# A hybrid attention layer on one core: product tails, decay ranks and block sums in another order

## The chip, the core and the metric

The kernel runs on one core of a Trainium2 chip. A core has a matmul engine (PE, whose weight loads are shown as PEld), a vector engine (DVE), a scalar engine (ACT), a general engine (POOL), a queue engine (SP) that mostly issues DMAs, and 16 DMA engines. Every engine works through its own queue in order and waits on semaphores where it needs another's result. The metric is the device time of one execution in microseconds; lower is better. Three executions of the kernel before took 2083.85 to 2084.41 us, median 2084.07 us.

## What is computed

One layer, in float32, on 1024 tokens of width 1024: a half-step SwiGLU feed-forward (width 2816), a mixer, and a second half-step feed-forward, each followed by a scaled residual and a layer norm.

```
x = layer_norm(ALPHA * x + 0.5 * swiglu_ffn(x, ffn1...), ln1)
x = layer_norm(ALPHA * x + hybrid_mixer(x, ...), ln2)
x = layer_norm(ALPHA * x + 0.5 * swiglu_ffn(x, ffn2...), ln3)

swiglu_ffn: (silu(x @ w_gate) * (x @ w_up)) @ w_down
hybrid_mixer: proj = x @ w_in -> na_q, na_k, na_v, g_q, g_k, g_v, g_g, dec_f, dec_b, gates
  merged = sigmoid(gate_na) * (neighborhood_attention(na_q, na_k, na_v) @ w_branch_na)
         + sigmoid(gate_gla) * (gated_linear_attention(g_q, g_k, g_v, g_g, dec_f, dec_b) @ w_branch_gla)
  return merged @ w_out
```

The two decay ranks `dec_f` and `dec_b` are 16 columns of the input projection each; they feed the decay gates of the linear attention.

## The kernel before, in words

Tokens are kept transposed: eight blocks of 128 model columns by two halves (h = 0, 1) of 512 tokens. Every float32 operand is split into a rounded high part and a low rest (`split`: an ACT copy and a DVE subtraction), and every product is three matmuls per block: high x high, high x low, low x high.

**Two-by-two products.** Most of the feed-forward and of the input projection is done by a Strassen-Winograd scheme: seven products of half size instead of eight. The token side is the 2 x 2 block matrix b11, b12 (blocks 0 to 3, half 0 and 1) and b21, b22 (blocks 4 to 7). Its sums t1 = b12 - b11, t2 = b22 - t1, t3 = b22 - b12 and t4 = b21 - t2 are made once per stage by `sums_of(i)` for i = 0 to 3, one block of each of the four sums at a time: four DVE subtractions and four splits per call. The results are T[0] to T[3]. The weight side is made per item by `factors`: `a11`, `a12`, `a22`, `s1` to `s4`.

**The order on PE.** PE's queue is exactly the order in which the program text issues matmuls (a manual schedule for this engine). For the other engines a list scheduler orders the instructions by priority, which is program order, and moves those inside `hoist()` or `high_priority` forward by 100 places. A second, hand-kept clock (`at`, `run`) places norm and attention steps between matmul steps.

**`blocks` and `pairs`.** `blocks` (L565) makes the gate and up projections of the feed-forward tiles 2 to 21; `pairs` (L884) makes eight items of the input projection. Both pipeline items: for item n the order is a11, a12 | `s3` of item n-1 | `s1` x T[0], `s2` x T[1] | `a22` of item n-1 | `s4`. `s3` and `a22` accumulate into one bank X; between them DVE adds the bank to a saved value (L587 in `blocks`, L936 in `pairs`). For the last item the loop runs once more with no new item, so its `s3`, the DVE read and its `a22` follow one another. `dense` has four PSUM banks.

**`down`, `deferred`.** The down projection (L712) does the same for eight items (two groups of six row tiles, four m each), with `gather` (L681) as the DVE read. The `s1` and `s4` products of the last two items, m = 2 and 3, are put on a list `wait`; `deferred` (L758) runs them later, behind the first of the parts that handle the remaining tiles (`plain` over LAST, L653): both `s1`, then both `s4`. Ahead of `down`, `front` runs 16 products over four other tiles.

**Between FFN1 and the pairs.** `tok_major` (L857) makes the attention values token-major: eight tiles of 128 tokens, of 24 matmuls (L873 to L875) each. Tiles 0 to 3 read half 0 of the normalized tokens, tiles 4 to 7 half 1, whose norm is still being finished meanwhile: DVE applies it (L322, L323), ACT scales and rounds, POOL subtracts the low part (L412). Then come the sums and `decay_rank` (L959): per half 16 matmuls (L970 to L973) into one bank, a copy, an addition (L977), a split and three stores. Its weights are loaded, rounded and split (L964) at its start. Then `pairs` begins, and behind it neighbourhood attention (L1077 and L1079 scores, L1083 to L1088 softmax, L1097 transposes) among the matmuls of a second `tok_major`.

Of the kernel before, what the change touches and what calls it, by code (L numbers as in the profile page):

```python
# [1 line left out]

# [7 lines left out]
F32R = mybir.dt.float32r  # L10
BF16 = mybir.dt.bfloat16
U32 = mybir.dt.uint32
AF = mybir.ActivationFunctionType
ALU = mybir.AluOpType
# [4 lines left out]
P = 128  # L19
D = 1024  # L20
S = 1024
KD = D // P
# [45 lines left out]
def hybrid_layer(ctx, tc, xT, wg1, wu1, wds1, wd1, wg2, wu2, wds2, wd2, wcol, wnv, wgv, wdl, wgate,  # L68
                 wbr, wout, lnp, bias, dec2, bdec, ng, ident_d, masks_d, ln3, outN):
    nc = tc.nc  # L70
# [56 lines left out]
    def dps(shape=(P, HF)):  # L127
        return dense.tile(list(shape), F32, tag="d", name=nm("d"))

    def split(src, hi, lo):  # L130
        nc.scalar.activation(hi, src, AF.Copy)  # L131
        nc.vector.tensor_tensor(lo, src, hi.bitcast(F32), ALU.subtract)  # L132
# [4 lines left out]
    def atile(dt=F32):  # L137
        return apool.tile([P, HF], dt, tag="a", name=nm("a"))
# [23 lines left out]
    for c1 in FIRST:  # L162
        w = slice(c0 * P, c1 * P)
# [25 lines left out]
    def run(*streams):  # L189
        for st_ in streams:  # L190
            for cost in st_:
                clock[0] += cost
                while pending and pending[0][0] <= clock[0]:
                    pending.pop(0)[2]()
# [6 lines left out]
    def hoist():  # L201
        return tc.high_priority(offset=HOIST)
# [228 lines left out]
    class Ffn:  # L431
# [16 lines left out]
                    self.hp.tile([P, HF], F32R, tag="hl", name=nm("hl")))  # L448


        def sums_of(self, i):
            b11, b12 = self.xr[i]
            b21, b22 = self.xr[i + 4]
            t1, t2, t3, t4 = (self.sr() for _ in range(4))
            outs = [self.hpair(), self.hpair()]
            nc.vector.tensor_tensor(t1, b12, b11, ALU.subtract)
            split(t1, *outs[0])
            nc.vector.tensor_tensor(t2, b22, t1, ALU.subtract)
            split(t2, *outs[1])
            nc.vector.tensor_tensor(t3, b22, b12, ALU.subtract)  # L460
            nc.vector.tensor_tensor(t4, b21, t2, ALU.subtract)
            outs += [(atile(F32R), atile(F32R)) for _ in range(2)]
            split(t3, *outs[2])
            split(t4, *outs[3])
            for n in range(4):
                self.T[n][i] = outs[n]


        def glu(self, f, ws, h):
# [95 lines left out]
        def blocks(self, fs):  # L565
            x, T = self.x, self.T
            b11, b21, b22 = ([x[k + o][h] for k in range(4)]
                             for o, h in ((0, 0), (4, 0), (4, 1)))
            prev = None
            for f in [*fs, None]:  # L570
                if f is not None:
                    w = self.factors(self.wg[f], self.wu[f])
                    X = dps()
                    yield from self.product(X, w["a11"], b11, True)
                    s1 = self.tmp()
                    with hoist():
                        nc.scalar.activation(s1, X, AF.Copy)
                    Y = dps()
                    yield from self.product(Y, w["a12"], b21, True)
                    with hoist():  # L580
                        nc.vector.tensor_tensor(s1, Y, s1, ALU.add)
                        nc.scalar.activation(s1, s1, AF.Silu)
                if prev:
                    g, pX, p1, p2, p5, pw = prev
                    yield from self.product(pX, pw["s3"], T[2])
                    with hoist():
                        nc.vector.tensor_tensor(p5, pX, p5, ALU.add)  # L587
                        nc.vector.tensor_tensor(p2, p2, p5, ALU.mult)
                    self.hidden(g, 1, p2)
                if f is not None:  # L590
                    Z = dps()
                    yield from self.product(Z, w["s1"], T[0], True)
                    s5 = self.tmp()
                    with hoist():
                        nc.scalar.activation(s5, Z, AF.Copy)
                    yield from self.product(X, w["s2"], T[1])
                    s2 = self.tmp()
                    with hoist():
                        nc.scalar.activation(s2, X, AF.Copy)
                if prev:  # L600
                    yield from self.product(pX, pw["a22"], T[3])
                    with hoist():
                        nc.vector.tensor_tensor(p1, pX, p1, ALU.mult)
                    self.hidden(g, 0, p1)
                if f is not None:
                    yield from self.product(Z, w["s4"], b22)
                    with hoist():
                        nc.vector.tensor_tensor(s2, Z, s2, ALU.add)
                        nc.scalar.activation(s2, s2, AF.Silu)
                    prev = f, X, s1, s2, s5, w  # L610


        def operands(self, j0):
# [98 lines left out]
        def down(self):  # L712
            prev, B, nxt = None, None, self.operands(0)
            self.wait = []
            items = [(j0, m) for j0 in range(0, PAIRS, NP) for m in range(4)]
            for it in [*items, None]:
                if it:
                    j0, m = it
                    if m == 0:
                        B, nxt = nxt, None  # L720
                    w = self.down_factors(j0, m)
                    if m == 1:
                        if j0 + NP < PAIRS:
                            nxt = self.operands(j0 + NP)
                        else:
                            for f in LAST:
                                self.fetch(f, 0)
                    X = dps()
                    yield from self.product(X, w["a11"], B[0], True)
                    self.gather(2 * m, 0, X)  # L730
                    Y = dps()
                    yield from self.product(Y, w["a12"], B[1], True)
                    self.gather(2 * m, 0, Y)
                if prev:
                    pm, pX, pw, pB = prev
                    yield from self.product(pX, pw["s3"], pB[5])
                    self.gather(2 * pm + 1, 1, pX)
                late = it and j0 + NP == PAIRS and m > 1
                if late:
                    self.wait.append((m, w, B))  # L740
                elif it:
                    Z = dps()
                    yield from self.product(Z, w["s1"], B[3], True)
                    self.gather(2 * m + 1, 1, Z)
                if it:
                    yield from self.product(X, w["s2"], B[4])
                    self.gather(2 * m, 1, X)
                if prev:
                    yield from self.product(pX, pw["a22"], pB[6])
                    self.gather(2 * pm + 1, 0, pX)  # L750
                if it:
                    if not late:
                        yield from self.product(Z, w["s4"], B[2])
                        self.gather(2 * m, 1, Z)
                    prev = m, X, w, B


        def deferred(self):  # L758
            banks = []
            for m, w, B in self.wait:  # L760
                banks.append(dps())
                yield from self.product(banks[-1], w["s1"], B[3], True)
                self.gather(2 * m + 1, 1, banks[-1])
            for Z, (m, w, B) in zip(banks, self.wait):
                yield from self.product(Z, w["s4"], B[2])
                self.gather(2 * m, 1, Z)

# [5 lines left out]
        def go(self, first, parts, sink_of):  # L773
# [5 lines left out]
                w2.append(ws)  # L779
            for f in (0, 1):  # L780
                run(self.glu(f, w2[f], 1))
            for i in range(4):
                self.sums_of(i)
            run(self.blocks(range(head, FT)))
            self.front()
            run(self.down())
# [1 line left out]
            sums = tagged(self.hp, ("sr",), 4)  # L788
# [33 lines left out]
    one = Ffn(ffn1, x, xr, half(xT), wg1, wu1, wds1, wd1, 0)  # L822
# [61 lines left out]
    def pairs(mb, items, each, last):  # L884
# [31 lines left out]
        for it in [*items, None]:  # L916
# [15 lines left out]
            if prev:  # L932
                g, pX, p5, pw = prev
                yield from mb.product(pX, pw["s3"], T[2])
                with hoist():
                    nc.vector.tensor_tensor(p5, pX, p5, ALU.add)  # L936
                store(g[3], 1, p5)
            if it:
                Z = dps()
# [10 lines left out]
                with hoist():  # L950
                    store(g[3], 0, pX, mb.tmp())
            if it:
                yield from mb.product(Z, w["s4"], b22)
                with hoist():
                    nc.vector.tensor_tensor(s2, Z, s2, ALU.add)
                store(it[2], 1, s2)
                prev = it, X, s5, w

    def decay_rank():  # L959
        raw = wpool.tile([P, KD, 32], F32, tag="raw", name=nm("raw"), bufs=2)  # L960
# [19 lines left out]
            for i, t in enumerate((hi, lo, hi)):  # L980
                nc.sync.dma_start(dls[32 * i:32 * i + 32, h * HF:(h + 1) * HF], t[0:32])

    run(tok_major(wnv, lambda t: vscr[t * P:(t + 1) * P, :], one.hpair))
    assert not pending
    x1h = [[x1[k][h] for k in range(KD)] for h in range(2)]
    one.x, one.xr = x1, x1r
    for i in range(4):
        one.sums_of(i)
    run(decay_rank())
    wq = []  # L990


# [527 lines left out]
```

## Time and profile before

| what | before |
|---|---|
| median of three runs | 2084.07 us |
| profiled execution | 2085.47 us |
| its span (first to last instruction) | 2083.6 us |
| matmuls | 9722 |
| PE busy | 2048.2 us |
| DVE busy | 1382.0 us |
| ACT busy | 898.5 us |
| POOL busy | 165.4 us |
| DMA moved | 321.37 MB |

Line numbers (L559) are lines of the kernel before. In a timeline the columns are start, duration, engine, line, operation and tiles, and in brackets the idle time just before and what ended it. Matmuls overlap: one is drawn as 0.39 us, though the next may start long before it ends, so a loss of time is best read from the distance of the starts. In a table of stretches the columns are the stretch, its length, busy time and number of instructions of PE, PEld, DVE, ACT and POOL, the granted clock of PE as a share of full speed, the busy share of the DMA engines and GB/s. In the list of waits they are total, number and longest.

### The profile page before, as it was taken

What the parts mean: (1) busy time and instruction counts of PE and PEld (TensorE: products, weight loads), DVE (VectorE), ACT (ScalarE), POOL (GpSimd) and SP (SyncE); (2) the same over time, 40 slices, a digit from 0 to 9 for tenths busy, and PEclk for the clock granted to TensorE, in tenths of its full rate; (3) what the DMA queues carried; (4) which work ended last, traced back from release to release, by engine and by line L of the source; (5) the groups of instructions that cost most, each with busy time, mean ns of one, the idle gap of its engine ahead of it and who ended that gap; (6) DMA issues with size and microseconds to landing.
All of it is one profiled execution on the core that took longest, in us unless ns stands there. A gap on an engine that the chain in (4) does not pass through costs nothing.

```text
span 2083.6 us, 26748 instructions
## 1 busy us (share of the span) xinstructions
PE 2048.2 (98%) x9722; PEld 1684.4 (81%) x9722; DVE 1382.0 (66%) x2356; ACT 898.5 (43%) x1503; POOL 165.4 (8%) x252
## 2 busy tenths in 40 slices
PE   9999999999999999989999999999999999999997
PEld 7888888888888788867778888887888888888887
DVE  8676776457668965236557765799767776457647
ACT  6444444322224654336655544455544444312222
POOL 0000000000013221222100000033000000000001
PEclk9999999999999999999999999999999999999999
DMA  4443444396641354477553335422334443496622
GB/s 145 147 155 141 167 142 138 125 312 216 220 136 55 108 199 145 128 194 228 160 139 106 107 127 182 142 81 71 137 137 152 165 160 120 126 333 216 236 90 82
DMA packets 159764, 321.37 MB, mean 154 GB/s; under 512 B 18448, under 2 KB 42768, under 8 KB 159632
## 3 DMA queue, kind: packets, MB, share of 16 engines
q1 hardware_dynamic: 139664, 271.93, 38.7%
q0 software_dynamic: 9856, 31.47, 5.3%
q10 hardware_dynamic: 10112, 16.26, 2.5%
q8 instruction: 77, 1.26, 0.2%
q14 instruction: 55, 0.45, 0.1%
HBM read 222.19 MB, written 101.06 MB: 155 GB/s over the span
## 4 chain that ended last, share of the span: by engine, by line
PE 84%; issue 6%; DVE 4%; DMA 2%; POOL 2%; ACT 1%; SPq 0%; ACTq 0%; POOLq 0%; DVEq 0%
PE d L559 16%; PE d L561 16%; PE d L560 16%; PE d L122 6%; PE d L124 6%; PE d L123 6%; PE d L660 3%; PE d L661 3%; PE d L659 3%; PE pt L1097 1%; PE po L1114 1%; DMA gv<-sl 1%; PE d L875 1%; PE d L874 1%; PE d L873 1%
## 5 line engine op out<-in xcount | busy, mean ns | idle before, releaser
L131 ACT ACTIVATE wh<-raw 128x512 fp32r<-128x512 f32 (+4 forms) x148 | 111.7, 764 | 191.8 <-PE d L560 87.0
L132 DVE TENSOR_TENSOR wl<-raw,wh 128x512 fp32r<-128x512 f32 (+4 forms) x148 | 125.2, 854 | 102.0 <-ACT wh L131 101.8
L681 DVE TENSOR_TENSOR a<-a,d 128x512 f32<-128x512 f32 (+1 forms) x152 | 100.0, 658 | 90.3 <-PE d L561 60.7
L123 PE MATMUL d<-xl,wh 128*128 128x512 f32 x384 | 150.6, 392 | 3.6 <-POOL xl L412 3.1
L122 PE MATMUL d<-xh,wh 128*128 128x512 f32 x384 | 153.6, 400 | 0.5 <-ACT xh L131 0.3
L559 PE MATMUL d<-a,wh 128*128 128x512 f32 x384 | 149.8, 390 | 2.4 <-DVE hr L587 1.6
L124 PE MATMUL d<-xh,wl 128*128 128x512 f32 x384 | 150.4, 392 | 0.5 <-DVE wl L112 0.5
L561 PE MATMUL d<-hh,hl 128*128 128x512 f32 x384 | 149.5, 389 | 0.0
L561 PE MATMUL d<-xh,wl 128*128 128x512 f32 x384 | 149.5, 389 | 0.0
L560 PE MATMUL d<-a,wh 128*128 128x512 f32 x384 | 149.4, 389 | 0.0
L561 PE MATMUL d<-a,wl 128*128 128x512 f32 x384 | 149.4, 389 | 0.0
L560 PE MATMUL d<-xl,wh 128*128 128x512 f32 x384 | 149.4, 389 | 0.0
L560 PE MATMUL d<-hl,hh 128*128 128x512 f32 x384 | 149.4, 389 | 0.0
L559 PE MATMUL d<-xh,wh 128*128 128x512 f32 x384 | 149.4, 389 | 0.0
L559 PE MATMUL d<-hh,hh 128*128 128x512 f32 x384 | 149.4, 389 | 0.0
L131 ACT ACTIVATE hh<-sr 128x512 fp32r<-128x512 f32 x168 | 106.1, 632 | 83.0 <-DVE sr L500 23.8
L659 PE MATMUL d<-hh,wh 128*128 128x512 f32 (+1 forms) x368 | 134.3, 365 | 0.0
L661 PE MATMUL d<-hh,wl 128*128 128x512 f32 (+1 forms) x368 | 133.0, 361 | 0.0
L660 PE MATMUL d<-hl,wh 128*128 128x512 f32 (+1 forms) x368 | 133.0, 361 | 0.0
L132 DVE TENSOR_TENSOR hl<-sr,hh 128x512 fp32r<-128x512 f32 x168 | 115.0, 698 | 2.0 <-ACT hh L131 1.2
L112 DVE TENSOR_TENSOR wl<-raw,wh 128x512 fp32r<-128x512 f32 (+1 forms) x77 | 81.2, 1054 | 51.8 <-ACT wh L111 46.1
L111 ACT ACTIVATE wh<-raw 128x512 fp32r<-128x512 f32 (+1 forms) x77 | 67.7, 879 | 103.4 <-PE d L123 38.3
(335 smaller groups left out, 4901.2 us busy)
## 6 DMA issues: line engine op xcount, KB each, us to landing
raw<-in_wu SPq DMA_DIRECT2D x44, 512.0 KB
raw<-in_wg SPq DMA_DIRECT2D x43, 512.0 KB
ops<-oh SPq DMA_DIRECT2D x84, 256.0 KB
ops<-ol SPq DMA_DIRECT2D x84, 256.0 KB
oh<-ops SPq DMA_DIRECT2D x48, 256.0 KB
ol<-ops SPq DMA_DIRECT2D x48, 256.0 KB
hid<-oh SPq DMA_DIRECT2D x40, 256.0 KB
hid<-ol SPq DMA_DIRECT2D x40, 256.0 KB
```

The source lines that it names most:

```text
L122: nc.tensor.matmul(ps, a, xh, start=k == 0, stop=False)
L123: nc.tensor.matmul(ps, a, xl, start=False, stop=False)
L124: nc.tensor.matmul(ps, wl[:, k * m:(k + 1) * m], xh, start=False, stop=k == n - 1)
L131: nc.scalar.activation(hi, src, AF.Copy)
L132: nc.vector.tensor_tensor(lo, src, hi.bitcast(F32), ALU.subtract)
L559: nc.tensor.matmul(ps, a, xh, start=first and k == 0, stop=False, **sg)
L560: nc.tensor.matmul(ps, a, xl, start=False, stop=False, **sg)
L561: nc.tensor.matmul(ps, wl[:, k * P:(k + 1) * P], xh, start=False, stop=k == n - 1, **sg)
L659: nc.tensor.matmul(ps, wh, hi, start=k == 0, stop=False)
L660: nc.tensor.matmul(ps, wh, lo, start=False, stop=False)
L661: nc.tensor.matmul(ps, wl, hi, start=False, stop=k == n - 1)
L681: nc.vector.tensor_tensor(a, a, ps, ALU.add)
```

## The change

Four orders are changed; no product is added or removed.

1. `sums()` replaces `sums_of(i)`: all four blocks of T[0] are made first, then T[1], T[2], T[3]. t2 takes its buffers from the tag `hr` (seven buffers) instead of `sr` (four).
2. In `blocks` and `pairs` the `s4` product of the last item, with its addition (and silu or store), is issued in the extra pass, between the last `s3` with its DVE read and the last `a22`.
3. In `down` of the second feed-forward (`self.idx` is 2 there and 0 in the first) the `s1` product of the last item, m = 3, is issued between the last `s3` and the last `a22`. `deferred` then runs `s1` of m = 2, `s4` of m = 3, `s4` of m = 2.
4. The 16 decay matmuls of half 0, with the load of their weights, are issued between token tiles 3 and 4. `islice` stops the generator at its eighth step, so what follows the matmuls of half 0 (copy, addition, split, stores) is issued where it was, behind the sums.

```diff
-        def sums_of(self, i):
...
+        def sums(self):
+            V, T, ks = nc.vector, self.T, range(4)
+            b11, b12 = ([self.xr[i][h] for i in ks] for h in range(2))
+            b21, b22 = ([self.xr[i + 4][h] for i in ks] for h in range(2))
+
+            def less(n, a, b, alloc):
+                out = []
+                for i in ks:
+                    out.append(alloc())
+                    V.tensor_tensor(out[i], a[i], b[i], ALU.subtract)
+                    T[n][i] = self.hpair() if n < 2 else (atile(F32R), atile(F32R))
+                    split(out[i], *T[n][i])
+                return out
+            t1 = less(0, b12, b11, self.sr)
+            t2 = less(1, b22, t1, self.tmp)
+            less(2, b22, b12, self.sr)
+            less(3, b21, t2, self.sr)
...
                     with hoist():
                         nc.vector.tensor_tensor(p5, pX, p5, ALU.add)
+                    if f is None:
+                        yield from third()
+                    with hoist():
                         nc.vector.tensor_tensor(p2, p2, p5, ALU.mult)
...
                 if f is not None:
-                    yield from self.product(Z, w["s4"], b22)
-                    with hoist():
-                        nc.vector.tensor_tensor(s2, Z, s2, ALU.add)
-                        nc.scalar.activation(s2, s2, AF.Silu)
                     prev = f, X, s1, s2, s5, w
+
+                    def third(Z=Z, w=w, s2=s2):
+                        yield from self.product(Z, w["s4"], b22)
+                        with hoist():
+                            nc.vector.tensor_tensor(s2, Z, s2, ALU.add)
+                            nc.scalar.activation(s2, s2, AF.Silu)
+                    if f != fs[-1]:
+                        yield from third()
...
                     yield from self.product(pX, pw["s3"], pB[5])
                     self.gather(2 * pm + 1, 1, pX)
+                    if not it and self.idx:
+                        yield from self.late_s1(self.wait[-1])
...
+        def late_s1(self, item):
+            m, w, B = item[:3]
+            Z = dps()
+            item.append(Z)
+            yield from self.product(Z, w["s1"], B[3], True)
+            self.gather(2 * m + 1, 1, Z)
...
         def deferred(self):
...
+            done = [item for item in self.wait if len(item) > 3]
+            todo = [item for item in self.wait if len(item) == 3]
+            for item in todo:
+                yield from self.late_s1(item)
+            for m, w, B, Z in done + todo:
                 yield from self.product(Z, w["s4"], B[2])
                 self.gather(2 * m, 1, Z)
...
-    run(tok_major(wnv, lambda t: vscr[t * P:(t + 1) * P, :], one.hpair))
+    tm, dr = tok_major(wnv, lambda t: vscr[t * P:(t + 1) * P, :], one.hpair), decay_rank()
+    run(islice(tm, 4 * KD), islice(dr, KD), tm)
...
-    for i in range(4):
-        one.sums_of(i)
-    run(decay_rank())
+    one.sums()
+    run(dr)
```

`pairs` changes as `blocks` does, with stores in place of the silu; in `go` the four calls of `sums_of` become one of `sums`.

More of the change, by code (lines that the diff above doesn't have):

```diff
@@ L1 @@
 from contextlib import ExitStack
+from itertools import islice
 import numpy as np
@@ L448, in hpair @@
                     self.hp.tile([P, HF], F32R, tag="hl", name=nm("hl")))
-        def sums_of(self, i):
[L452 to L466, printed above, removed]
+        def sums(self):
[14 more added lines that the diff above has]
+            less(3, b21, t2, self.sr)
         def glu(self, f, ws, h):
@@ L737, in down @@
                     self.gather(2 * pm + 1, 1, pX)
+                    if not it and self.idx:
+                        yield from self.late_s1(self.wait[-1])
                 late = it and j0 + NP == PAIRS and m > 1
                 if late:
-                    self.wait.append((m, w, B))
+                    self.wait.append([m, w, B])
                 elif it:
@@ L755, in down @@
                     prev = m, X, w, B
-        def deferred(self):
[L759 to L764, printed above, removed]
+        def late_s1(self, item):
[4 more added lines that the diff above has]
+            self.gather(2 * m + 1, 1, Z)
+        def deferred(self):
+            done = [item for item in self.wait if len(item) > 3]
[3 more added lines that the diff above has]
+            for m, w, B, Z in done + todo:
                 yield from self.product(Z, w["s4"], B[2])
@@ L781, in go @@
                 run(self.glu(f, w2[f], 1))
-            for i in range(4):
-                self.sums_of(i)
+            self.sums()
             run(self.blocks(range(head, FT)))
@@ L936, in pairs @@
                     nc.vector.tensor_tensor(p5, pX, p5, ALU.add)
+                if not it:
+                    yield from third()
                 store(g[3], 1, p5)
@@ L952, in pairs, with third @@
             if it:
[L953 to L956, printed above, removed]
                 prev = it, X, s5, w
+                def third(Z=Z, w=w, s2=s2, out=it[2]):
+                    yield from mb.product(Z, w["s4"], b22)
+                    with hoist():
+                        nc.vector.tensor_tensor(s2, Z, s2, ALU.add)
+                    store(out, 1, s2)
+                if it is not items[-1]:
+                    yield from third()
     def decay_rank():
@@ L986, in hybrid_layer @@
     one.x, one.xr = x1, x1r
-    for i in range(4):
-        one.sums_of(i)
-    run(decay_rank())
+    one.sums()
+    run(dr)
     wq = []
```

## The prediction

> **What bounds the kernel now.** I read the page's busy shares first, then the waits of the matmul engine, then its timeline around each wait that the change touches, then the timelines of DVE, POOL and SP there.
>
> ```profile
> PE 2048.2 (98%) x9722; PEld 1684.4 (81%) x9722; DVE 1382.0 (66%) x2356; ACT 898.5 (43%) x1503; POOL 165.4 (8%) x252
> ```
>
> PE's matmuls are busy for 98% of the span and the next engine, DVE, for 66%, so there are 35.4 us (2083.6 - 2048.2) of PE idleness to win and little else, as long as no matmul is removed; the change removes none. What it can do is fill waits. These are PE's longest (total, times, longest, in us):
>
> ```profile
> PE pt L1097 <- DVE e L1088: 4.8, 3, 4.3
> PE d L123 <- POOL xl L412: 3.1, 4, 1.2
> PE d L875 <- POOL xl L412: 2.2, 3, 0.7
> PE d L559 <- DVE a L681: 1.7, 2, 0.9
> PE d L559 <- DVE hr L587: 1.6, 2, 0.8
> PE d L559 <- DVE hr L936: 0.8, 1, 0.8
> ```
>
> Four of the six are touched. L875 is a token tile that reads half 1 of the normalized tokens before POOL has made them. The three L559 rows are product tails: `s3` accumulates into a bank, DVE reads the bank (L681, L587, L936), and only then may `a22` accumulate into it; nothing stands between the two at the end of a chain. The listed idleness understates each loss, since a matmul is drawn 0.39 us long while the next starts far sooner. So I price losses by start times. The undisturbed step is:
>
> ```profile
> 725.67 0.39 PE L559 MATMUL d<-hh,hh 128*128 128x512 f32 x1
> ...
> 728.39 0.39 PE L559 MATMUL d<-hh,hh 128*128 128x512 f32 x1
> ```
>
> These are twelve steps, one product of four blocks: 2.72 us, 0.227 us each.
>
> **The change part by part.** *Last items of `blocks` (both FFNs) and `pairs`.* The `s4` product of the last item moves from before `s3` to between `s3` and `a22`. The count of instructions is the same.
>
> ```profile
> 431.74 0.39 PE L561 MATMUL d<-a,wl 128*128 128x512 f32 x1
> ...
> 435.80 0.39 PE L659 MATMUL d<-hh,wh 128*128 128x512 f32 x1
> ```
>
> ```profile
> 869.60 0.39 PE L561 MATMUL d<-a,wl 128*128 128x512 f32 x1
> ...
> 873.67 0.39 PE L873 MATMUL d<-wh,xh 128*128 128x512 f32 x1
> ```
>
> From the last `s3` matmul to the first one behind `a22` is 4.06 us in FFN1 and 4.07 us in the pairs, against 13 steps = 2.95: losses of 1.11 and 1.12 us. FFN2 has the second of the two L587 waits, and I take 1.11 again. The moved product lasts 2.72 us, far over the gap it has to cover, so all three go: 3.34 us. The step that was pulled forward, `s3`, still has the previous item's `a22` (2.72 us) between it and the ACT copy of its bank. The new wait: p2 = s2 * p5 now needs the silu behind `s4`, and its two stores queue on SP behind it about a microsecond later; what they hold up is loads of the down stage's operands, needed only after the front part's 16 products (16 x 2.72 = 43.5 us). In `pairs` two stores swap on POOL's queue; the last one, from `a22`, stays last. Cost nothing; without those covers it would be that one microsecond.
>
> *Deferred products.* In FFN2 the `s1` product of m = 3 moves from behind the first LAST part into the tail of `down`.
>
> ```profile
> 1985.23 0.39 PE L561 MATMUL d<-oh,wl 128*128 128x512 f32 x1
> ...
> 1988.42 0.40 PE L561 MATMUL d<-oh,wl 128*128 128x512 f32 x1
> ```
>
> 3.19 us for nine steps (2.04): 1.15 us lost, and a nine-matmul product of 2.04 us covers it. What remains deferred is `s1`(2), `s4`(3), `s4`(2): one product still lies between `s1`(2) and `s4`(2), so no new wait. One of four dense banks is held through eight products of 18 matmuls (4.1 us each); three suffice. FFN1 keeps its 0.9.
>
> *Half 0's decay rank.* Its 16 matmuls move ahead of token tile 4.
>
> ```profile
> 690.63 0.39 PE L873 MATMUL d<-hh,xh 128*128 128x512 f32 x1
> ...
> 696.16 0.50 PE L875 MATMUL d<-hh,xl 128*128 128x512 f32 x1 [0.71 <-POOL xl L412]
> 696.50 0.39 PE L873 MATMUL d<-wh,xh 128*128 128x512 f32 x1
> ```
>
> ```profile
> 716.29 0.39 PE L973 MATMUL d<-xl,wh 128*64 128x512 f32 x1
> ...
> 719.98 0.39 PE L973 MATMUL d<-xl,wh 128*64 128x512 f32 x1
> ```
>
> The last four steps of tile 4 take 5.87 us instead of 2.72: 3.15 us lost to POOL. One decay half lasts 3.69 us (end of half 0 to end of half 1). Put ahead, it needs half 0 only. Tile 4 then starts not at 687.9 (690.63 less four blocks of 0.68) but at 691.6, and reads its last block at 691.6 + 7 x 0.68 + 0.45 = 696.8; POOL had that block ready at 696.16, 0.6 us sooner. So 3.15 us go. The inserted matmuls need their weights, and the chain of waits and the DVE timeline say when they come:
>
> ```profile
> 664.25 0.68 DVE wh L964
> 719.27 0.69 DVE L132 TENSOR_TENSOR a<-sr,a 128x512 fp32r<-128x512 f32 x1
> 720.47 1.26 DVE L977 TENSOR_TENSOR sl<-sl,d 32x512 f32<-32x512 f32 x2
> ```
>
> L964 ends 23 us ahead of tile 4, although its code stands behind all tiles: the load on SP, the cast and the subtraction run early already. The epilogue (ACT copy, L977, split, three `dls` stores on SP) is still issued behind the sums, so SP's order around the regrouping hardly moves. Half 0's bank is now held through tiles 4 to 7. By 720.47 + 1.26 = 721.7 it is free, and the fourth bank after it is wanted at 725.67 - 3.15 = 722.5: 0.8 us of slack; if the vector engine runs later than that, the excess is lost.
>
> *Sums by block.* The same 48 instructions, in another order. Before, the last of them ends at 719.27 + 0.69 = 720.0, and the `s1` product first reads T[0] at 725.67; after, at 722.5. Even the old order would be in time by 2.5 us, and the new one finishes T[0] first. Worth nothing here by itself. It is a hedge for the shorter cover. What it may cost is in the last rival. t2 lives in `hr` (7 buffers) instead of `sr`, which leaves `sr` to the factors sooner.
>
> **Sum.** 3.34 + 1.15 + 3.15 = 7.64 us. The profiled execution took 2085.47 us with a span of 2083.6 (1.9 us around it), so it would take 2077.8, span 2076.0. It lies 1.4 us above the median of the three runs, 2084.07; from that, the forecast is 2076.4.
>
> **The rivals.** *First: the start of neighbourhood attention answers.* Behind the pairs PE waits for loads and for ACT, and its clock falls:
>
> ```profile
> 875.59 2.82 DMA ogs<-hr
> 880.82 22.04 DMA gv<-sl
> ```
>
> ```profile
> 901.00:906.50 5.50, 1.19 (x4) 0.43 (x2) 1.00 (x4) 3.16 (x6) 0.00 (x0) 0.51 0.25 92
> 906.50:912.00 5.50, 5.50 (x18) 4.68 (x19) 1.35 (x5) 2.03 (x6) 0.00 (x0) 0.55 0.32 101
> ```
>
> A 22 us store holds ACT, ACT holds `e`, `e` holds PE (4.3 us), and 5.5 us run at a clock of 0.55. All of it starts from the pairs' end, so it should move along unchanged. But t2's new tag changes which `hr` buffer the last store reads, and the next stage's tiles lie on that memory: a load that did not wait for the 2.82 us of that store may now do so. Bounds: 2.5 us better (5.5 x 0.45, the slow clock gone) to 5.3 worse (2.82 of wait and another 2.5 of slow clock): 2073.9 to 2081.7, middle of the worse side 2079.2. For it: a congested spot (a store of 22 us). Against it: nothing there is reordered. The Trainium skill (TensorE: Matmul & The Clock Gate, Part 1) has the clock halved after an idle window of about 3.4 us; by that rule the trace agrees here (0.51), and the waits of about 1 us that this change removes never cost clock. The chances below do not use it.
>
> *Second: the moved decay half hides nothing,* as POOL's chain or the bank slips along with it. Then 3.15 us stay: 2079.6. For it: slacks of 0.6 and 0.8 us. Against: both would have to be missed by 3 us.
>
> *Third: the tails keep their waits,* if the list scheduler puts DVE's read of the bank behind the moved product's own reads. Then 4.49 us (3.34 + 1.15) stay: 2080.9. Against: those reads are hoisted and in program order ahead of the moved product.
>
> *Fourth, on the other side: the port between DVE and POOL.* In FFN2 the same stall on POOL (L123, 3.1 us) has no decay half in front of it.
>
> ```profile
> 1402.11 1.30 POOL L412 TENSOR_TENSOR xl<-a,xh 128x512 fp32r<-128x512 f32 x1 [5.02 <-ACT xh L411]
> 1433.07 1.00 DVE L456 TENSOR_TENSOR sr<-a,a 128x512 f32<-128x512 f32 x1
> 1433.99 0.67 DVE L323 TENSOR_TENSOR a<-a,pl 128x512 f32<-128x512 f32 x1
> 1435.68 1.76 DVE L132 TENSOR_TENSOR hl<-sr,hh 128x512 fp32r<-128x512 f32 x1
> 1427.17 11.40 POOL L412 TENSOR_TENSOR xl<-a,xh 128x512 fp32r<-128x512 f32 x8 [6.03 <-ACT xh L411]
> ```
>
> One subtraction of the sums (L456) already runs ahead of the norm's last step (L323). In block order all of T[0] needs only blocks 0 to 3, normalized first; if its eight DVE operations ran ahead of the last L323 at 1.76 us each, PE would wait 8 x 1.76 - 1.00 = 13.1 us longer: 2089.5. From five of them on (5 x 1.76 - 1.00 = 7.8) the whole gain is gone. Against it: L456 needs block 0 alone, the first to be normalized, and yet 15 of the 16 steps of L322 and L323 went ahead of it. The Trainium skill (SBUF — State Buffer, Who interferes with whom) says that a DVE instruction with two SBUF inputs and a GpSimd one that reads SBUF lock each other out, which speaks against bringing such subtractions forward. By that rule the trace agrees: 1.76 us against 0.67 for a step that reads PSUM. The other end: with no contention POOL's eight blocks would take 8 x 1.30 = 10.4 instead of 11.40 us, a gain of 1.0. I take 0, the same few operations meeting the same few blocks.
>
> **How the numbers follow.** Forecast 0.66, first rival 0.15 (0.05 better, 0.10 worse), second 0.10, third 0.05, fourth 0.04. About 0.2%, 4.2 us, is what a measurement of this kernel can tell from no change: the line lies at 2079.9. Faster: 0.66 + 0.05, half of the second (0.05, it sits on the line) and half of the first's worse side (0.05): 0.81. Slower: most of the fourth, 0.03. The rest, 0.16, within. The range runs from 2072.9 (first rival's better end and the 1.0 us of the port) to 2081.7 (its worse end); the third lies inside, the fourth outside.
>
> **What would show it.** Right: L587 and L936 gone from PE's waits, L681 once instead of twice, L875 gone, PE's busy time unchanged within 1 us, and tile 4 in steps of 0.227 us. The L123 row stays near 3.1 and pt L1097 near 4.8; these two are what would make the sum wrong without any of its terms failing. Wrong: an L559 wait on ACT or on a bank in the tails, a wait at the pairs' first `s1` product, or a decay matmul waiting for `wh`.

## The result, and the profile after

The changed kernel takes 2110.77 us (median of 4 executions, 2109.84 to 2111.63) against 2083.99 us of the kernel before on the same chip (2083.85 to 2084.41): a ratio of 1.0126, 95% interval 1.0112 to 1.014. It is 27 us slower where 7.6 us of gain were forecast. The profiled execution took 2109.84 us with a span of 2108.1. Line numbers from here on are those of the kernel named; in the changed kernel a product is L561 to L563 (before: L559 to L561), a split L132 and L133, the sums L461, the glu result L481, the factors L502 to L509.

The page of the kernel after, its matmul row:

```profile
PE 2053.3 (97%) x9722; PEld 1688.6 (80%) x9722; DVE 1379.9 (65%) x2356; ACT 898.0 (43%) x1503; POOL 165.0 (8%) x252
```

As many instructions as before on every engine. PE is busy 5.1 us longer (2053.3 against 2048.2) for the same matmuls: some ran at a lower clock, as the last section shows behind two of the waits. The other 19.4 us of the span's 24.5 are waits. The longest of PE's waits after (total, times, longest):

```profile
PE d L561 <- ACT hh L132: 21.1, 2, 10.5
PE d L561 <- ACT hr L942: 4.1, 1, 4.1
PE pt L1119 <- DVE e L1110: 3.9, 3, 3.5
PE d L124 <- POOL xl L413: 3.1, 4, 1.2
PE s L1101 <- DMA kl<-qks: 2.9, 1, 2.9
```

The rows that the change aimed at (L587, L936, L875, one of the two L681) are gone. In their place stand two waits of 10.5 us for `hh` and one of 4.1 us. PE's timeline shows the first in FFN1's first item; the second, in FFN2, looks the same:

```profile
59.27 0.39 PE L563 MATMUL d<-xh,wl 128*128 128x512 f32 x1
70.19 0.79 PE L561 MATMUL d<-hh,hh 128*128 128x512 f32 x1 [10.54 <-ACT hh L132]
...
74.21 0.39 PE L561 MATMUL d<-hh,hh 128*128 128x512 f32 x1
```

```profile
1485.71 0.80 PE L561 MATMUL d<-hh,hh 128*128 128x512 f32 x1 [10.54 <-ACT hh L132]
```

`hh` is the split of `s1`, the first weight factor of the item. DVE's timeline says why it is late. After, with the last block of t1 (`sr<-a,a`), the second to fourth glu result (L481) and the first blocks of t2:

```profile
27.52 0.69 DVE L461 TENSOR_TENSOR sr<-a,a 128x512 f32<-128x512 f32 x1
...
32.49 0.69 DVE L481 TENSOR_TENSOR hr<-d,sl 128x512 f32<-128x512 f32 x1 [2.48 <-PE d L125]
...
43.44 0.69 DVE L481 TENSOR_TENSOR hr<-d,sl 128x512 f32<-128x512 f32 x1 [3.36 <-PE d L125]
...
54.25 0.69 DVE L481 TENSOR_TENSOR hr<-d,sl 128x512 f32<-128x512 f32 x1 [2.27 <-PE d L125]
54.86 1.29 DVE L461 TENSOR_TENSOR hr<-a,sr 128x512 f32<-128x512 f32 x2
...
68.19 0.68 DVE L461 TENSOR_TENSOR sr<-a,hr 128x512 f32<-128x512 f32 x1
68.80 0.68 DVE L502 TENSOR_TENSOR sr<-raw 128x512 f32<-128x512 f32 x1
```

Before:

```profile
46.36 0.69 DVE L500 TENSOR_TENSOR sr<-raw 128x512 f32<-128x512 f32 x1
```

DVE makes the fourth and last glu result at 54.25 and t2 (`hr<-a,sr`) directly behind it, though it idled for 2.27 us just before and though the last block of t1 was done at 28.2. Until then t1 holds all four `sr`; then t3 and t4 pass through `sr`, and `s1` of the factors comes at 68.80 instead of 46.36, 22.4 us later.

Where the time went, stage by stage (distance between the first matmuls of consecutive stages, us):

| stage | before | after | difference |
|---|---|---|---|
| `blocks`, FFN1 | 381.92 | 393.49 | +11.57 |
| token tiles and decay ranks | 57.02 | 53.86 | -3.16 |
| `pairs` | 153.46 | 159.11 | +5.65 |
| start of neighbourhood attention (second `tok_major`) | 79.11 | 77.48 | -1.63 |
| rest of the mixer, FFN2 up to its `blocks` | 502.77 | 504.16 | +1.39 |
| `blocks`, FFN2 | 382.36 | 393.95 | +11.59 |
| `down` and `deferred`, FFN2 (without the LAST part between them) | 117.18 | 116.05 | -1.13 |

They add up to +24.3 of the span's +24.5.

### The profile page after: what moved, and what is told of

It is laid out like the page before. It is cut to its first block, busy times and chain, and to the rows that moved or that the text cites. A ratio compares the mean times of both kernels' runs of the same rounds, so it can differ in the third digit from the quotient of the medians.

```text
span 2108.1 us, 26776 instructions
## 1 busy us (share of the span) xinstructions
PE 2053.3 (97%) x9722; PEld 1688.6 (80%) x9722; DVE 1379.9 (65%) x2356; ACT 898.0 (43%) x1503; POOL 165.0 (8%) x252
## 4 chain that ended last, share of the span: by engine, by line
PE 80%; DVE 7%; issue 7%; DMA 3%; ACT 1%; POOL 1%; ACTq 0%; SPq 0%; DVEq 0%; POOLq 0%
PE d L561 16%; PE d L562 16%; PE d L563 16%; PE d L123 5%; PE d L124 5%; PE d L125 5%; PE d L670 3%; PE d L668 3%; PE d L669 3%; PE pt L1119 1%; PE po L1136 1%; DMA gv<-sl 1%; DMA sb<-gts 1%; DVE sr L461 1%; POOL qks L905 1%
## 5 line engine op out<-in xcount | busy, mean ns | idle before, releaser
L133 DVE TENSOR_TENSOR wl<-raw,wh 128x512 fp32r<-128x512 f32 (+4 forms) x148 | 125.2, 853 | 111.3 <-ACT wh L132 111.2
L132 ACT ACTIVATE wh<-raw 128x512 fp32r<-128x512 f32 (+4 forms) x148 | 111.6, 763 | 197.9 <-PE d L562 85.0
L561 PE MATMUL d<-hh,hh 128*128 128x512 f32 x384 | 152.4, 397 | 25.2 <-ACT hh L132 21.1
L563 PE MATMUL d<-hh,hl 128*128 128x512 f32 x384 | 151.7, 395 | 0.0
L561 PE MATMUL d<-xh,wh 128*128 128x512 f32 x384 | 149.4, 389 | 0.0
L563 PE MATMUL d<-xh,wl 128*128 128x512 f32 x384 | 149.4, 389 | 0.0
L561 PE MATMUL d<-a,wh 128*128 128x512 f32 x384 | 149.4, 389 | 0.0
L563 PE MATMUL d<-a,wl 128*128 128x512 f32 x384 | 149.4, 389 | 0.0
L132 ACT ACTIVATE hh<-sr 128x512 fp32r<-128x512 f32 x156 | 97.9, 630 | 75.2 <-PE d L562 25.0
L132 ACT ACTIVATE oh<-hr 128x512 fp32r<-128x512 f32 x88 | 55.5, 631 | 134.3 <-DVE hr L593 45.0
```

Source lines behind the costliest of these rows:

```text
L561: nc.tensor.matmul(ps, a, xh, start=first and k == 0, stop=False, **sg)
L563: nc.tensor.matmul(ps, wl[:, k * P:(k + 1) * P], xh, start=False, stop=k == n - 1, **sg)
```

## The experiments

The four parts of the change were first taken apart, then the suspected buffer, then a second finding. Times are medians beside the kernel before on the same chip, ratios with their 95% intervals.

| kernel | us | ratio | FFN1 `blocks` | tokens, decay | `pairs` | attention's start | FFN2 `blocks` |
|---|---|---|---|---|---|---|---|
| before | 2084.0 to 2084.7 | 1 | 381.92 | 57.02 | 153.46 | 79.11 | 382.36 |
| changed | 2110.77 | 1.0126 | 393.49 | 53.86 | 159.11 | 77.48 | 393.95 |
| e1_old_sums | 2069.78 | 0.9931 (0.9919 to 0.9944) | 380.80 | 53.86 | 153.83 | 69.70 | 381.19 |
| e2_sums_only | 2106.01 | 1.0106 (1.0092 to 1.012) | 394.64 | 57.02 | 154.67 | 73.71 | 395.96 |
| e3_decay_only | 2083.06 | 0.9992 (0.9983 to 1.0001) | 381.90 | 53.86 | 154.79 | 78.51 | 382.15 |
| e4_tails_only | 2073.36 | 0.9947 (0.9935 to 0.996) | 380.83 | 56.99 | 152.34 | 71.64 | 381.17 |
| e5_hr_ahead | 2109.65 | 1.0121 (1.0107 to 1.0135) | 393.29 | 53.87 | 159.17 | 77.57 | 393.83 |
| e6_in_place | 2068.46 | 0.9924 (0.9912 to 0.9936) | 380.80 | 53.87 | 152.34 | 69.97 | 381.19 |
| e7_other_buffer | 2084.65 | 0.9999 (0.999 to 1.0008) | 381.89 | 57.02 | 153.44 | 78.65 | 382.30 |
| e8_tail_ffn1 | 2079.88 | 0.9976 (0.9967 to 0.9985) | 380.80 | 57.28 | 153.54 | 77.73 | 381.13 |
| e9_glu_sl | 2076.39 | 0.996 (0.9946 to 0.9973) | 381.86 | 53.88 | 159.91 | 69.29 | 381.24 |
| e10_between | 2077.77 | 0.997 (0.9959 to 0.998) | 380.80 | 53.86 | 159.35 | 71.63 | 382.78 |
| e11_last_store | 2074.76 | 0.9954 (0.994 to 0.9968) | 381.90 | 57.02 | 153.46 | 68.20 | 382.33 |
| e12_both | 2067.45 | 0.9918 (0.9904 to 0.9931) | 380.80 | 53.86 | 152.34 | 68.23 | 381.19 |

**e1_old_sums**: the changed kernel, with the sums made block by block as before.

```diff
-            self.sums()
+            for i in range(4):
+                self.sums_of(i)
```

> The changed kernel with the sums again one block of all four at a time (t2 in sr), everything else as changed. Stage lengths in the two traces say: blocks +11.6 us in each FFN, token tiles -3.2, pairs +5.7, the rest within 2 us. Theory A (buffer queue): the sums by block are the whole loss in the FFNs, since t2 takes buffers of the tag hr, which are given out in program order, behind the last result of glu. Then both 10.5 us waits of the first s1 product are gone: 2078 us if the 4.1 us wait in the pairs comes from the sums as well (A1), 2085 us if it comes from half 0's decay matmuls having left their epilogue behind (A2). Rival B (the new tails or closures hold something the first item needs): the waits stay, 2105 us or more.

Measured 2069.78 us: 41 us off the changed kernel by one part undone. The three waits go, and 30.7 us with them in `blocks` and `pairs`, more than the whole loss: it came from the part that was priced at nothing. It is also 8 us faster than A1's 2078, and the table says where: attention's start takes 69.70 us instead of 77.48 in the changed kernel (79.11 before). One new wait of PE stands in the `pairs`:

```profile
PE d L560 <- DVE sl L919: 1.2, 1, 1.2
```

**e2_sums_only**: the kernel before, with `sums` in place of `sums_of`.

```diff
-            for i in range(4):
-                self.sums_of(i)
+            self.sums()
```

> The kernel before with only the sums by block. Theory A: two stalls of 12.7 us (10.7 of wait and 2.0 at half clock): 2109.4 us with A2, and 2116 us with A1, where the pairs stall too. Rival B: 2084 us, no new wait.

Measured 2106.01 us: both feed-forwards lose 12.7 and 13.6 us, the pairs only 1.2. So the 5.65 us in the changed kernel's pairs need the moved decay half as well, and neither A1 nor A2 is right about them. Attention's start is 5.40 us shorter here, with nothing but the sums changed.

**e3_decay_only**: the kernel before, with the decay half moved.

```diff
-    run(tok_major(wnv, lambda t: vscr[t * P:(t + 1) * P, :], one.hpair))
+    tm, dr = tok_major(wnv, lambda t: vscr[t * P:(t + 1) * P, :], one.hpair), decay_rank()
+    run(islice(tm, 4 * KD), islice(dr, KD), tm)
```

> The kernel before with only half 0's decay matmuls ahead of token tile 4. A1 (the pairs' wait comes from the sums): the token stage is 3.15 us shorter and nothing else moves, 2080.8 us. A2 (the epilogue of half 0, left behind the tiles, queues with that of half 1 and delays the copy of the pairs' first bank): 3.15 us won, 6.8 lost, 2087.6 us.

Measured 2083.06 us, 1.4 us less, at the edge of what can be told. The token tiles gain their 3.16 us, but the pairs give 1.33 back; A2's loss of 6.8 us does not come.

**e4_tails_only**: the kernel before, with the tails (here that of `pairs`) and `deferred` changed.

```diff
+                if not it:
+                    yield from third()
                 store(g[3], 1, p5)
```

> The kernel before with only the last items of blocks and pairs and the deferred s1 reordered. My step: four waits of 1.11 to 1.15 us go, 4.5 us in all: 2079.5 us. The rival that the tails keep their waits: 2084 us.

Measured 2073.36 us, 11 us less instead of 4.5. The three tails bring 1.09, 1.12 and 1.19 us; attention's start brings 7.47 more, though nothing in that stage is reordered.

**e5_hr_ahead**: the four `hr` buffers of t2 requested ahead of the glu calls.

```diff
+            self.t2 = [self.tmp() for _ in range(4)]
             w2 = []
...
-            t2 = less(1, b22, t1, self.tmp)
+            t2 = less(1, b22, t1, lambda: self.t2.pop(0) if self.t2 else self.tmp())
```

> The changed kernel, with the four `hr` buffers of t2 requested ahead of the glu calls of each feed-forward instead of behind them; no instruction is added, removed or reordered in the program text. Theory A1 (a buffer of a tag is given in the order of the requests, so t2 stands behind the four glu results, t1 keeps the four `sr` meanwhile, and the factors get theirs 22 us late): both 10.5 us waits for `hh` go, blocks FFN1 and FFN2 come back from 393.5 and 393.9 to about 380.8 and 381.2 us; the pairs have no glu ahead and keep their 4.1 us wait. 2110.8 - 12.7 - 12.8 = 2085, or 2078 if the start of neighbourhood attention takes its faster form too. Rival (seven `hr` buffers are too few for four t2 and four glu results): the waits stay or grow, 2110 or more.

Measured 2109.65 us: nothing moved, and the theory in this form fell. The rival named, too few buffers, forecast about this time, but the rows of the changed kernel speak against it: until 54.25 us only three glu results had been written to `hr` (at 22.78, 32.49 and 43.44), so four of its seven buffers had never been written while t2 waited. DVE's timeline of this kernel:

```profile
53.75 0.69 DVE L481 TENSOR_TENSOR hr<-d,sl 128x512 f32<-128x512 f32 x1 [2.27 <-PE d L125]
54.35 1.29 DVE L461 TENSOR_TENSOR hr<-a,sr 128x512 f32<-128x512 f32 x2
```

Where a buffer is requested does not count. The next form of the theory: what counts is where it is first written.

**e6_in_place**: sums still by block, no `hr` used.

```diff
...
-            t1 = less(0, b12, b11, self.sr)
-            t2 = less(1, b22, t1, self.tmp)
-            less(2, b22, b12, self.sr)
-            less(3, b21, t2, self.sr)
+            t = less(0, b12, b11, [self.sr() for i in ks])
+            less(1, b22, t, t)
+            less(3, b21, t, t)
+            less(2, b22, b12, [self.sr() for i in ks])
```

> The changed kernel, sums still by block, but t2 written over t1 and t4 over t2 in the four `sr` buffers, t3 last: no `hr` buffer is used, 48 instructions as before. Theory A1 (only the `hr` tag hurts, the order by block is neutral): no `hh` wait in the feed-forwards, no 4.1 us wait in the pairs, time as with the old sums, 2069.8 (2067 to 2072). Rival A2 (the pairs' wait comes from the order by block, which puts the decay half behind DVE work of the first factors, not from `hr`): the feed-forwards come back, the pairs stay at 159.1 us instead of 153.8: 2075.

Measured 2068.46 us. DVE's timeline: t2 written over t1 (`sr<-a,sr`) from 28.39, `s1` of the factors at 44.57:

```profile
28.39 0.69 DVE L459 TENSOR_TENSOR sr<-a,sr 128x512 f32<-128x512 f32 x1
...
44.57 0.68 DVE L500 TENSOR_TENSOR sr<-raw 128x512 f32<-128x512 f32 x1
```

All three waits are gone with the order by block kept, so that order is harmless. (e6 makes t4 ahead of t3, as in-place writing needs; that the tag does the harm in the feed-forwards is shown by e9 below, which leaves the sums as they are.) The rival that blamed the order for the pairs' wait falls too: 152.34 us there, and neither the give-back of e1 nor that of e3.

**e9_glu_sl** and **e10_between** test the second form, each with t2 in `hr`: glu gives up its `hr`, or the sums are called between the second and third glu call.

```diff
-                hr = self.tmp()
-                nc.vector.tensor_tensor(hr, pu, sl, ALU.mult)
-            self.leave(self.hs[f, h], hr)
+                nc.vector.tensor_tensor(sl, pu, sl, ALU.mult)
+            self.leave(self.hs[f, h], sl)
```

```diff
                 w2.append(ws)
+            self.sums()
             for f in (0, 1):
                 run(self.glu(f, w2[f], 1))
-            self.sums()
```

> The changed kernel (t2 in `hr`), with the four glu results written over their silu in `sl` instead of into an `hr` buffer of their own: glu takes no `hr` any more, nothing else changes. Theory A3 (a buffer of a tag is given in the order of the first writes in the program; t2's first write stands behind the four glu results, and that puts it behind the last of them in DVE's queue): t2 runs before 40 us, both 10.5 us waits for `hh` go, the two blocks stages take about 381 us, time 2110.8 - 25.5 = 2085 with the pairs' 4.1 us wait kept, and 2078 if the last store of the pairs comes to lie off the first bias tile. Rival (t2 runs late because of its place in the order by block, whatever buffers glu uses): the waits stay, 2103 or more.

> The changed kernel, with the call of the sums moved between the first two and the last two glu calls; same instructions and buffers. Theory A3: t2's first writes now stand behind two glu results instead of four, so t2 runs right behind the second result (32 us in the first feed-forward instead of 54), the factors get `sr` 22 us sooner, both `hh` waits go: 2085, or 2078 with the faster start of neighbourhood attention. Rival (order by block): 2103 or more. Risk: the sums now stand ahead of work that the second half of the norm in front of the second feed-forward needs; if so the wait on POOL (3.1 us) grows.

Measured 2076.39 and 2077.77 us. DVE's timeline of e9, t2 at 29.13 and `s1` at 45.31:

```profile
29.13 0.68 DVE L461 TENSOR_TENSOR hr<-a,sr 128x512 f32<-128x512 f32 x1
...
45.31 0.68 DVE L501 TENSOR_TENSOR sr<-raw 128x512 f32<-128x512 f32 x1
```

And of e10, t2 directly behind the second glu result instead of the fourth:

```profile
32.35 0.69 DVE L481 TENSOR_TENSOR hr<-d,sl 128x512 f32<-128x512 f32 x1 [2.62 <-PE d L125]
32.95 1.89 DVE L461 TENSOR_TENSOR hr<-a,sr 128x512 f32<-128x512 f32 x3
...
49.17 0.68 DVE L502 TENSOR_TENSOR sr<-raw 128x512 f32<-128x512 f32 x1
```

In both the two `hh` waits are gone and the pairs keep theirs (4.5 and 4.1 us), as expected of a stage that has no glu. Each has about a microsecond of new waits: e9's FFN1 `blocks` take 381.86 us (0.7 on ACT, L599), e10's FFN2 `blocks` 382.78 (1.7 on DVE, L133). e10 keeps PE's wait on POOL ahead of FFN2 at 3.1 us: the risk named for it did not come.

**e7_other_buffer** and **e11_last_store** are about attention's start, both on the kernel before. e7 requests one more `hr` buffer ahead of the pairs' last store and leaves it unused; e11 keeps that last value in `sl`.

```diff
+                    if not it:
+                        mb.tmp()
                     store(g[3], 0, pX, mb.tmp())
```

```diff
-                    store(g[3], 0, pX, mb.tmp())
+                    store(g[3], 0, pX, mb.tmp() if it else stage())
```

> The kernel before, with one more `hr` buffer requested and left unused ahead of the last store of the pairs, so that this store reads another of the seven buffers; nothing else. Theory B (the 7 us that the tails alone gained beyond their 4.5 come from the start of neighbourhood attention: where the last store reads a buffer that the bias tiles of the next stage lie on, ACT waits 2.8 us for the store, and the value stores behind it land late): the stage from the pairs' end to the gate products goes from 79.1 to 70-74 us, the score wait on DVE (4.3 us) and the half clock go, 2084.5 - 6 = 2078 (2075 to 2080). Rival (the gain comes from the store of s2 leaving earlier, or from the tail being shorter): 2084.5, stage 79.1.

> The kernel before, with the last value that the pairs store kept in an `sl` buffer instead of `hr`; nothing else. `sl` is not overlaid by tiles of the next stage. Theory B (the first bias load of neighbourhood attention waits for that store, since its tile lies on the buffer that the store reads, and ACT's queue, the value stores, the scores and the clock follow): the first bias load is issued within 1 us of the stage's start instead of 4.8 us behind it, the stage takes 70 to 72 us instead of 79.1, time 2084.7 - 8 = 2077 (2075 to 2079). Rival (the faster form comes from the order of the last stores or from the shorter tail): 2084.7.

e7 measured 2084.65 us, no difference, and the first bias load still waits. By the reading of e5 a buffer that is never written is not given out, so e7 says nothing about the theory; that its last store reads the same buffer as before is not shown. e11 measured 2074.76 us: 9.5 us for one tag in one line, a little more than theory B's 8. ACT's timeline before, the first issues behind the pairs' end at 873.67 (`bt` a bias tile, `gv` a value tile stored):

```profile
878.51 1.21 ACTq L1060 DMA_DIRECT2D bt<-in_bias  x2
...
880.82 0.97 ACTq L879 DMA_DIRECT2D gv<-sl  x1
...
893.46 0.33 ACTq L879 DMA_DIRECT2D gv<-sl  x1
```

In e11, where the stage begins at 873.71:

```profile
873.99 0.42 ACTq L1060 DMA_DIRECT2D bt<-in_bias  x1
...
875.26 0.91 ACTq L1060 DMA_DIRECT2D bt<-in_bias  x2
...
879.98 0.33 ACTq L879 DMA_DIRECT2D gv<-sl  x1
...
885.42 0.33 ACTq L879 DMA_DIRECT2D gv<-sl  x1
```

The first bias load no longer stands behind the landing of the last store (875.59 + 2.82 = 878.41), the second value store leaves 8 us sooner, and PE's clock stays up. Five us of it by stretch in e11:

```profile
900.00:905.00 5.00, 5.00 (x37) 4.11 (x36) 2.61 (x10) 2.53 (x8) 0.00 (x0) 1.00 0.13 45
```

and five of the changed kernel's, with the wait and the half clock:

```profile
915.00:920.00 5.00, 1.50 (x7) 0.77 (x5) 0.87 (x5) 3.50 (x7) 0.00 (x0) 0.50 0.18 66
```

All kernels of the table fall into place by this. Where the first bias load waits for the last store (before, changed, e3, e5, e7, e8) it is issued 4.7 to 5.0 us behind the stage's start and the stage takes 77.5 to 79.1 us; where another load waits, or none (e1, e2, e4, e6, e9 to e12), 0.3 to 1.6 us behind it, and the stage takes 68.2 to 73.7. In e4, for one, the third bias load waits and the first leaves at once:

```profile
871.76 0.42 ACTq L1082 DMA_DIRECT2D bt<-in_bias  x1
...
873.03 0.35 ACTq L1082 DMA_DIRECT2D bt<-in_bias  x1
...
878.19 0.39 ACTq L1082 DMA_DIRECT2D bt<-in_bias  x1
```

So the extra 7 us of e4 and the 8 of e1 are an accident. The likely reason is that with the last stores reordered the last one reads another of the seven `hr` buffers, on which another bias tile lies. That is argued from which load waits; no view shows the addresses.

**e8_tail_ffn1**: e1, with FFN1's `down` tail filled as FFN2's.

```diff
-                    if not it and self.idx:
+                    if not it:
```

> The changed kernel with the old sums, and the `s1` product of the last `down` item pulled into the tail of the first feed-forward too (there the 0.9 us wait on the gather was kept). Tail theory: 1.1 us less than with the old sums alone, 2069.8 - 1.1 = 2068.7, no wait on the gather left. Rival (the first feed-forward has something else behind that tail, so that the product only moves the wait): 2069.8 as before.

Measured 2079.88 us, 10 us more than e1. The tail gains its 0.9 us (114.51 us for `down` and `deferred`, 115.40 in e1), and two other places answer: attention's start falls back to 77.73 us (its first bias load waits again), and the token tiles up to the moved decay half take 28.13 us instead of 24.73. They now start about 1 us earlier and run into the norm: a wait of 1.8 us on POOL and a clock of 0.72 over the 5 us around it. One of PE's waits and a stretch of this kernel:

```profile
PE d L891 <- POOL xl L413: 1.8, 1, 1.8
```

```profile
667.00:672.00 5.00, 3.52 (x10) 2.78 (x11) 4.76 (x6) 1.12 (x2) 1.43 (x2) 0.72 0.20 30
```

**e12_both**: e6 and e11 together.

> A version that should beat both kernels: the changed kernel with t2 and t4 written in place in `sr`, and the last store of the pairs from `sl`. With the sums in place alone it is 2068.5, and there the third bias load still waits for the last store (at 6.7 us behind the stage's start). Theory B: that wait goes as well, the stage is at most 1 us shorter: 2067.5 to 2068.5. Rival (the `sl` buffer is missed by the value tiles of the next stage, which use it): 2070 or more.

Measured 2067.45 us, ratio 0.9918 (0.9904 to 0.9931): the fastest kernel here, 16.8 us under the kernel before and 43 under the changed one.

## Why the prediction was wrong

The step that failed is the one on the sums: "Worth nothing here by itself", with "t2 lives in `hr` (7 buffers) instead of `sr`, which leaves `sr` to the factors sooner". It counted instructions and capacity and not who stands ahead of t2 in that tag. In these kernels t2 runs directly behind the last writer of `hr` that stands ahead of it in the program, as if the buffers of a tag were given out in the order of their first writes: not the request counts (e5), nor the free buffers, but the writers ahead (e9 takes them away, e10 halves them). In both feed-forwards these are the four glu results, which wait for PE. So t2 ran behind the last of them, t1 kept `sr`, and in FFN1 the factors came 22.4 us later, not sooner. Price against e6: 12.7 us in FFN1 (11.57 beside the 1.1 that the tail gained), 12.8 in FFN2 and 6.8 in the pairs. Together that is 32.3 us; the profiled execution missed its forecast of 2077.8 by 32.0.

*The tails and `deferred`*: right. 1.09 to 1.19 us for each of three tails (forecast 1.11, 1.12, 1.11), 1.13 for `deferred` (1.15). No new wait from p2, the silu or the stores.

*The decay half*: right in its place, 3.16 us (3.15), and the "0.8 us of slack" behind it was too small a worry: e3 gives 1.33 us back in the pairs, e1 1.49. The stage starts 3.9 us earlier in e1 (716.30 against 720.21), its fourth pair of weight loads does not (741.44 and 741.87 against 740.47 and 741.64), and DVE's read of a bank (L919) behind those factors comes late. e6 has the moved half and no such wait; which order of DVE avoids it was not taken apart.

*The sum*: with the sums out of the way, the five terms give 1.12 + 3.16 + 1.12 + 1.17 + 1.13 = 7.70 us in e12 against 7.64 in the prediction.

*The first rival* named a real mechanism, a bias load that waits for the last store or not, and was too small in size. In the changed kernel it did not come: the first bias load still waits, and the stage is only 1.63 us shorter. But the new sums alone do what the rival says (e2: first bias load 0.35 us behind the stage's start, stage 5.40 us shorter), the tails alone do it too (e4), and the two together bring the wait back. Its better end took only the half clock away (2.5 us); the waits of scores and ACT go too, and the stage gains 5.4 to 10.9 us. So "nothing there is reordered" was no argument against it. (The middle of its worse side is 2079.05, not 2079.2; no chance changes by that.)

*The second and third rival* did not come. *The fourth* did not either: the wait on POOL ahead of FFN2 is 3.1 us before, after and in every other kernel, and in e10 with the sums further ahead.

*What would show it*: the four named waits went, as said. Wrong was to look for failures only in the tails and at the pairs' first `s1`: two of the new waits are at the first `s1` of `blocks`, and the pairs' is one product further on, at the first `s2`. PE's busy time rose by 5.1 us, beyond the 1 us allowed, and that row alone pointed to a lower clock.

What stays open is the pairs' own wait. The first item's `s2` accumulates into the bank X, which ACT has to copy first. ACT's timeline after has that copy (L942) right behind the split of the second decay half:

```profile
740.00 0.63 ACT L132 ACTIVATE hr<-sl 32x512 fp32r<-32x512 f32 x1 [0.56 <-DVE sl L999]
740.65 0.60 ACT L942 ACTIVATE hr<-d 128x512 f32<-128x512 f32 x1
```

and DVE's has the addition that this split needs (L999, the second of two) behind the second item's factors, 9 us behind the first:

```profile
730.28 0.68 DVE L999 TENSOR_TENSOR sl<-sl,d 32x512 f32<-32x512 f32 x1
...
738.10 0.68 DVE L509 TENSOR_TENSOR sr<-raw,raw 128x512 f32<-128x512 f32 x1
...
739.30 0.67 DVE L999 TENSOR_TENSOR sl<-sl,d 32x512 f32<-32x512 f32 x1
```

In e1, with the moved half and the old sums, the two additions stand 2.4 us apart (716.48 and 718.88), ahead of those factors. The split and the copy write `hr`, and it takes t2 in `hr` and the moved half together (e2 and e3 alone lose 1.2 and 1.3 us, both 5.65 beside a tail that gains 1.1). Whether t2's place among the writers of `hr`, or the number of its buffers, sets this chain is not shown: no run separates the two.

## What to carry to other kernels

A change of a buffer's tag is a change of order: before pricing it, list who writes that tag earlier in the program and what those writers wait for, since the number of buffers alone does not tell. Where stages overlay each other's memory, look up which buffer the last store of a stage reads and which load of the next stage lies on it; unrelated edits move that pairing, and each then seems to win or lose by it. Time the parts of a change separately: here -11, -1.4 and +21.5 us hid behind one number. And do not expect them to add up: they sum to +9.0, the whole is +26.8. Attention's start gains 7.5 us with the tails alone and 5.4 with the sums alone, but 1.6 with everything, and the pairs lose 5.65 us instead of 1.4.

## What was not expected of the hardware

The price of a wait is more than its length. Behind the first 10.5 us wait nine matmul steps took 4.02 us (70.19 to 74.21) instead of 9 x 0.227 = 2.04, so the wait cost 2 us more than it lasted; the 4.1 us wait was followed by as long a stretch (741.30 to 745.31). The two stretches of the changed kernel, with the granted clock in the third column from the end:

```profile
70.20:74.00 3.80, 3.80 (x9) 2.63 (x10) 3.80 (x7) 1.72 (x3) 0.00 (x0) 0.52 0.00 0
```

```profile
741.30:745.00 3.70, 3.70 (x9) 2.92 (x10) 2.06 (x4) 2.58 (x4) 0.58 (x1) 0.50 0.76 238
```

The Trainium skill (TensorE: Matmul & The Clock Gate, Part 1) has the clock halved after an idle window of about 3.4 us and restored after a busy one of that length; by that rule the trace agrees here, with 0.52 and 0.50 over 3.8 and 3.7 us, whether the wait was 10.5 or 4.1 us long, and 1.00 from 74.0 to 78.0.
